# A NaN-ignoring maximum over 512 MB: tiles cut into row pieces, stores moved to the load queue

## The chip, the core and the metric

The kernel runs on one core of one Trainium2 chip. Times are device microseconds of that core. Five engines run side by side, each with its own instruction queue: PE (unused here), ACT, DVE, POOL and SP, which issues the loads. Instructions wait for each other through semaphores.

## The reference

```python
def setup_inputs():
    batch, seq, dim = 32, 2048, 2048
    x = np.random.randn(batch, seq, dim).astype(np.float32)
    mask = np.random.rand(batch, seq, dim) < 0.1
    x[mask] = np.nan
    return {"x": x, "axis": -1}

def reference(x, axis):
    return np.nanmax(x, axis=axis).astype(np.float32)
```

65,536 rows of 2048 floats (8 KB a row, 536.87 MB in all) become 65,536 maxima; a tenth of the input is NaN.

## The kernel before

Each of the 128 partitions takes 512 rows. They are worked on in 14 groups (`GROUPS`): 12 groups of 40 rows a partition in five tiles of 8, one group of 24 (7, 6, 5, 4, 2), one of 8 (2, 2, 1, 1, 1, 1). A tile of 8 rows is 64 KB a partition, 8.39 MB. Tiles come from a pool of three buffers (`io`, `bufs=3`); a load into a buffer waits until the tile that was there is reduced.

A tile goes through four steps, each one instruction over the whole tile:

- SP issues the load (L74).
- ACT changes the upper 16 bits of each float in place, with a Prelu of the negated bits (L77). POOL subtracts the result from a constant, in place, and so brings the bits back (L85). Between them, the two map the upper halves of NaNs to those of a very low number and leave the others as they are.
- DVE takes the maximum of each row into `acc` (L93).

After a group's last tile DVE finds rows that had only NaN (`none`, L101) and puts the NaN back into the result (`fin`, L110); ACT's queue issues the group's store (L113). Each queue runs in the order in which its instructions stand. The framework that builds the program adds the semaphores, and places ACT's store of a group behind the first activation of the next group (the order below shows it).

Of the kernel before, what the change touches and what calls it, by code (L numbers as in the profile page):

```python
# [1 line left out]

# [4 lines left out]

GROUPS = [(40, [8] * 5)] * 12 + [
    (24, [7, 6, 5, 4, 2]),
    (8, [2, 2, 1, 1, 1, 1]),
]

TOP = 0x7F7F
NAN = 0x7FC0
LOW = -129  # L20

EDGE = TOP + 0.25

NONE = -255.0 * 2.0**120


@with_exitstack
def kernel(
    ctx: ExitStack,
    tc: tile.TileContext,  # L30
    x: bass.AP,
    axis: bass.AP,
    out: bass.AP,
):

    nc = tc.nc
    P = nc.NUM_PARTITIONS
    f32, i32 = mybir.dt.float32, mybir.dt.int32
    i16, u16 = mybir.dt.int16, mybir.dt.uint16
    ALU = mybir.AluOpType

    nd = len(x.shape)
    assert axis in (-1, nd - 1), axis  # L50
    D = x.shape[-1]

    xr = x.bitcast(i32).flatten_outer_dims()
    R = xr.shape[0]
    of = out.bitcast(i32).flatten_outer_dims().rearrange("r c -> (r c)")
    assert R == P * sum(s for s, _ in GROUPS)

    io = ctx.enter_context(tc.tile_pool(name="io", bufs=3))
    res = ctx.enter_context(tc.tile_pool(name="res", bufs=3))
    sing = ctx.enter_context(tc.tile_pool(name="sing", bufs=1))  # L60
    top = sing.tile([P, 1], f32)
    nc.vector.memset(top, EDGE)  # L62

    r0 = 0
    for s, cuts in GROUPS:
        assert sum(cuts) == s
        xg = xr[r0 : r0 + P * s].rearrange("(p s) d -> p s d", p=P)
        og = of[r0 : r0 + P * s].rearrange("(p s) -> p s", p=P)
        r0 += P * s
        acc = res.tile([P, s], f32, tag="acc")  # L70
        at = 0
        for c in cuts:
            xt = io.tile([P, c * D], i32, tag="xt")
            nc.sync.dma_start(  # L74
                out=xt, in_=xg[:, at : at + c].rearrange("p c d -> p (c d)")
            )
            nc.scalar.activation(  # L77
                out=xt.bitcast(u16)[:, 1::2],
                in_=xt.bitcast(i16)[:, 1::2],
                func=mybir.ActivationFunctionType.Prelu,  # L80
                bias=top,
                scale=-1.0,
                alpha=float(TOP - LOW) / (EDGE - NAN),
            )
            nc.gpsimd.tensor_scalar(  # L85
                out=xt.bitcast(i16)[:, 1::2],
                in0=xt.bitcast(u16)[:, 1::2],
                scalar1=-1.0,
                scalar2=float(TOP),
                op0=ALU.mult,  # L90
                op1=ALU.add,
            )
            nc.vector.tensor_reduce(  # L93
                out=acc[:, at : at + c],
                in_=xt.bitcast(f32).rearrange("p (c d) -> p c d", c=c),
                axis=mybir.AxisListType.X,
                op=ALU.max,
            )
            at += c
        none = res.tile([P, s], i32, tag="none")  # L100
        nc.vector.tensor_scalar(  # L101
            out=none,
            in0=acc,
            scalar1=NONE,
            scalar2=float(0x00C00000),
            op0=ALU.is_equal,
            op1=ALU.mult,
        )
        fin = res.tile([P, s], i32, tag="fin")
        nc.vector.tensor_tensor(  # L110
            out=fin, in0=acc.bitcast(i32), in1=none, op=ALU.bitwise_or
        )
        nc.scalar.dma_start(out=og, in_=fin)  # L113


# [1 line left out]
_INS = ['x', 'axis']  # L117
_OUTS = [((32, 2048), 'float32')]

_NUMBERS = {'axis': -1}  # L120


# [26 lines left out]
```

## Time and profile before

| | |
|---|---|
| median of 3 runs | 1747.19 us (1747.01 to 1747.41) |
| the profiled execution's own time | 1748.27 us |
| its span, first to last instruction | 1746.5 us |
| busy: ACT, POOL, DVE | 1182.0, 1174.7, 1143.4 us |
| read from HBM | 536.87 MB, 308 GB/s over the span |

A row of the timeline is: start, duration, engine, line, operation, out<-in, number of instructions, and in brackets the idle time ahead of it with what ended it. A row of groups: line, engine, operation, out<-in with shapes, count | busy us, mean ns of one | idle time before, what ended it. `128x16384` is a tile of 8 rows as ACT and POOL see it (upper halves alone), `128x8` its result on DVE. A row of waits: who waited for whom, us in total, times, longest. A row of windows: the window, its length, busy time of DVE, ACT and POOL, granted clock, DMA share, GB/s. A row of DMA issues: out<-in, queue, count, KB each, median us from issue to landing. "SPq" and "ACTq" are the queues of these engines.

### The profile page before, as it was taken

What the parts mean: (1) busy time and instruction counts of PE and PEld (TensorE: products, weight loads), DVE (VectorE), ACT (ScalarE), POOL (GpSimd) and SP (SyncE); (2) the same over time, 40 slices, a digit from 0 to 9 for tenths busy, and PEclk for the clock granted to TensorE, in tenths of its full rate; (3) what the DMA queues carried; (4) which work ended last, traced back from release to release, by engine and by line L of the source; (5) the groups of instructions that cost most, each with busy time, mean ns of one, the idle gap of its engine ahead of it and who ended that gap; (6) DMA issues with size and microseconds to landing.
All of it is one profiled execution on the core that took longest, in us unless ns stands there. A gap on an engine that the chain in (4) does not pass through costs nothing.

```text
span 1746.5 us, 655 instructions
## 1 busy us (share of the span) xinstructions
DVE 1143.4 (65%) x100; ACT 1182.0 (68%) x72; POOL 1174.7 (67%) x75
## 2 busy tenths in 40 slices
DVE  0568585585585585675674774864865856856886
ACT  4865956856857757758668668567577586586553
POOL 0959577587586585595595595595595595595854
DMA  9595976966967867868768669669569669569343
GB/s 420 234 444 246 385 308 269 385 282 294 385 264 312 361 263 338 334 268 360 313 264 384 293 260 408 265 263 429 241 267 410 265 264 428 245 264 411 142 192 144
DMA packets 12244, 537.17 MB, mean 308 GB/s; under 512 B 3152, under 2 KB 3152, under 8 KB 3152
## 3 DMA queue, kind: packets, MB, share of 16 engines
q1 hardware_dynamic: 10224, 536.88, 72.6%
q10 hardware_dynamic: 2016, 0.26, 0.1%
q14 instruction: 4, 0.03, 0.0%
HBM read 536.87 MB, written 0.26 MB: 308 GB/s over the span
## 4 chain that ended last, share of the span: by engine, by line
DVE 26%; POOL 26%; ACT 22%; DMA 19%; issue 6%; ACTq 0%; POOLq 0%; DVEq 0%
POOL xt L85 26%; DVE acc L93 24%; ACT xt L77 22%; DMA xt<-in_x_dram 19%; DVE none L101 2%; ACTq L113 0%; POOLq L144 0%; DVE fin L110 0%; ACTq L77 0%; POOLq L85 0%; DVEq L93 0%
## 5 line engine op out<-in xcount | busy, mean ns | idle before, releaser
L85 POOL TENSOR_SCALAR xt<-xt 128x16384 int16<-128x16384 uint16 (+4 forms) x71 | 1174.5, 16542 | 566.4 <-ACT xt L77 565.6
L77 ACT ACTIVATE xt<-xt,top 128x16384 uint16<-128x16384 int16 (+4 forms) x71 | 1180.7, 16642 | 533.8 <-DMA xt<-in_x_dram 323.1
L93 DVE TENSOR_REDUCE acc<-xt 128x8 f32<-128x16384 f32 (+4 forms) x71 | 1102.6, 15535 | 598.9 <-POOL xt L85 598.9
L101 DVE TENSOR_SCALAR none<-acc 128x40 int32<-128x40 f32 (+2 forms) x14 | 39.1, 2790 | 0.5
L77 ACT ACT_TABLE_LOAD x1 | 1.3, 1283 | 23.0 <-DMA xt<-in_x_dram 23.0
L110 DVE TENSOR_TENSOR fin<-acc,none 128x40 int32<-128x40 int32 (+2 forms) x14 | 2.8, 197 | 0.5
L62 DVE MEMSET top<- 128x1 f32 x1 | 0.1, 59 | 0.8 <-PEq L130 0.8
L130 POOL MEMSET const-float32-0.0<- 128x1 f32 x1 | 0.1, 98 | 0.2 <-issue 0.2
L130 POOL MEMSET const-bfloat16-1.0<- 128x1 bf16 x1 | 0.1, 102 | 0.0
L130 POOL MEMSET const-uint8-127<- 128x1 uint8 x1 | 0.1, 102 | 0.0
L130 POOL MEMSET const-float32-1.0<- 128x1 f32 x1 | 0.1, 98 | 0.0
## 6 DMA issues: line engine op xcount, KB each, us to landing
xt<-in_x_dram SPq DMA_DIRECT2D x1, 7168.0 KB, 19.6
xt<-in_x_dram SPq DMA_DIRECT2D x1, 6144.0 KB, 16.9
xt<-in_x_dram SPq DMA_DIRECT2D x3, 2048.0 KB, 7.3
xt<-in_x_dram SPq DMA_DIRECT2D x1, 5120.0 KB, 14.6
xt<-in_x_dram SPq DMA_DIRECT2D x1, 4096.0 KB, 12.0
xt<-in_x_dram SPq DMA_DIRECT2D x4, 1024.0 KB, 4.7
xt<-in_x_dram SPq DMA_DIRECT2D x60, 22.0
out_dram<-fin ACTq DMA_DIRECT2D x12, 20.0 KB, 19.6
```

The lines of the kernel that those rows point to most:

```text
L62: nc.vector.memset(top, EDGE)
L77: nc.scalar.activation(out=xt.bitcast(u16)[:, 1::2], in_=xt.bitcast(i16)[:, 1::2], func=mybir.ActivationFunctionType.Prelu, bias=top, scal ...
L85: nc.gpsimd.tensor_scalar(out=xt.bitcast(i16)[:, 1::2], in0=xt.bitcast(u16)[:, 1::2], scalar1=-1.0, scalar2=float(TOP), op0=ALU.mult, op1= ...
L93: nc.vector.tensor_reduce(out=acc[:, at : at + c], in_=xt.bitcast(f32).rearrange("p (c d) -> p c d", c=c), axis=mybir.AxisListType.X, op=A ...
L101: nc.vector.tensor_scalar(out=none, in0=acc, scalar1=NONE, scalar2=float(0x00C00000), op0=ALU.is_equal, op1=ALU.mult,)
L110: nc.vector.tensor_tensor(out=fin, in0=acc.bitcast(i32), in1=none, op=ALU.bitwise_or)
L130: nc = _bacc.Bacc("TRN2", target_bir_lowering=False, num_devices=1)
```

## The change

A group is now a list of tiles, a tile a list of loads, a load a list of pieces. The 60 tiles of the first 12 groups stay one load each, but ACT, POOL and DVE work on it in pieces of 3, 3 and 2 rows (`FULL`). The last 32 rows become four groups of one tile each: a full tile; a tile of three loads (2+2, 2, 2 rows); a tile of six loads (2, 2, 1, 1, 1, 1); a tile of eight loads of one row. Stores are kept in a list and issued on SP's queue behind a load, when at least two groups are done; what is left goes out at the end. A Prelu on one number a partition (`warm`) stands ahead of everything on ACT. The three instructions on a piece are those of before, on the view `xp` of its rows.

```diff
-GROUPS = [(40, [8] * 5)] * 12 + [
-    (24, [7, 6, 5, 4, 2]),
-    (8, [2, 2, 1, 1, 1, 1]),
+FULL = [[3, 3, 2]]
+GROUPS = [[FULL] * 5] * 12 + [
+    [FULL],
+    [[[2, 2], [2], [2]]],
+    [[[2], [2], [1], [1], [1], [1]]],
+    [[[1], [1], [1], [1], [1], [1], [1], [1]]],
 ]
+WIDE = 8
...
+    warm = sing.tile([P, 1], f32)
+    nc.scalar.activation(out=warm, in_=top, func=PRELU, alpha=0.5)
 
+    stores = []
...
-        for c in cuts:
-            xt = io.tile([P, c * D], i32, tag="xt")
-            nc.sync.dma_start(
-                out=xt, in_=xg[:, at : at + c].rearrange("p c d -> p (c d)")
-            )
...
+        for tl in g:
+            xt = io.tile([P, WIDE * D], i32, tag="xt")
+            base = at
+            for ld in tl:
+                c = sum(ld)
+                nc.sync.dma_start(
+                    out=xt[:, (at - base) * D : (at - base + c) * D],
+                    in_=xg[:, at * D : (at + c) * D],
+                )
+                if len(stores) > 1:
+                    nc.sync.dma_start(**stores.pop(0))
+                for c in ld:
+                    xp = xt[:, (at - base) * D : (at - base + c) * D]
...
+                    at += c
...
-        nc.scalar.dma_start(out=og, in_=fin)
+        stores.append(dict(out=og, in_=fin))
+    for st in stores:
+        nc.sync.dma_start(**st)
```

Three places show how instructions move. The first is ACT's queue from its start (`xt` is the tile, `fin` the result of a group of 40 rows). Before:

```order
L77 ACT_TABLE_LOAD
L77 ACTIVATE xt<-xt,top 128x16384 x6
L113 DMA out_dram<-fin 128x40
L77 ACTIVATE xt<-xt,top 128x16384 x5
L113 DMA out_dram<-fin 128x40
```

and changed:

```order
L71 ACT_TABLE_LOAD
L71 ACTIVATE warm_66<-top_64 128x1
L94 ACTIVATE xt_69<-xt_69,top_64 128x6144 x2
L94 ACTIVATE xt_69<-xt_69,top_64 128x4096
L94 ACTIVATE xt_80<-xt_80,top_64 128x6144 x2
L94 ACTIVATE xt_80<-xt_80,top_64 128x4096
```

The store is gone from between the activations, a tile is three activations, and the table load does not stand behind the first load any more.

The second is SP's queue at the end of the program. Before (the last loads; there is nothing else on the queue):

```order
L74 DMA xt<-in_x_dram 128x16384 x60
L74 DMA xt<-in_x_dram 128x14336
L74 DMA xt<-in_x_dram 128x12288
L74 DMA xt<-in_x_dram 128x10240
L74 DMA xt<-in_x_dram 128x8192
L74 DMA xt<-in_x_dram 128x4096 x3
L74 DMA xt<-in_x_dram 128x2048 x4
```

and changed, where `xt_799` is tile 60 (the tiles are counted from 0), `xt_816` tile 61, `xt_838` tile 62, `xt_869` tile 63, and `fin_796`, `fin_813`, `fin_835` are the results of the groups that end with tile 59, 60 and 61:

```order
L86 DMA xt_799<-in_x_dram 128x16384
L91 DMA out_0_dram<-fin_735 128x40
L86 DMA xt_816<-in_x_dram 128x8192
L91 DMA out_0_dram<-fin_796 128x40
L86 DMA xt_816<-in_x_dram 128x4096 x2
L86 DMA xt_838<-in_x_dram 128x4096 x2
L91 DMA out_0_dram<-fin_813 128x8
L86 DMA xt_838<-in_x_dram 128x2048 x4
L86 DMA xt_869<-in_x_dram 128x2048 x2
L91 DMA out_0_dram<-fin_835 128x8
L86 DMA xt_869<-in_x_dram 128x2048 x6
L132 DMA out_0_dram<-fin_866 128x8
```

Three stores now stand between loads, one tile or two behind the tile whose result they carry. (A load of 4 or 2 rows is one row here with 8192 or 4096 elements, 2048 a row.)

The third is DVE's queue at the same place, as changed:

```order
L127 TENSOR_TENSOR fin_796<-acc_737,none_794 128x40
L110 TENSOR_REDUCE acc_798<-xt_799 128x3 x2
L110 TENSOR_REDUCE acc_798<-xt_799 128x2
L110 TENSOR_REDUCE acc_815<-xt_816 128x2
L118 TENSOR_SCALAR none_811<-acc_798 128x8
L110 TENSOR_REDUCE acc_815<-xt_816 128x2
L127 TENSOR_TENSOR fin_813<-acc_798,none_811 128x8
L110 TENSOR_REDUCE acc_815<-xt_816 128x2 x2
L110 TENSOR_REDUCE acc_837<-xt_838 128x2
L118 TENSOR_SCALAR none_833<-acc_815 128x8
L110 TENSOR_REDUCE acc_837<-xt_838 128x2
L127 TENSOR_TENSOR fin_835<-acc_815,none_833 128x8
```

`none` and `fin` of a short group stand behind the first and the second reduce of the next tile, where before, with the last two groups,

```order
L93 TENSOR_REDUCE acc_438<-xt_459 128x2
L101 TENSOR_SCALAR none_464<-acc_438 128x24
L110 TENSOR_TENSOR fin_466<-acc_438,none_464 128x24
L93 TENSOR_REDUCE acc_469<-xt_470 128x2
L93 TENSOR_REDUCE acc_469<-xt_475 128x2
```

they stood right behind their own.

More of the change, by code (lines that the diff above doesn't have):

```diff
@@ L47 @@
     ALU = mybir.AluOpType
+    PRELU = mybir.ActivationFunctionType.Prelu
     nd = len(x.shape)
@@ L55 @@
     of = out.bitcast(i32).flatten_outer_dims().rearrange("r c -> (r c)")
-    assert R == P * sum(s for s, _ in GROUPS)
+    rows = [sum(sum(sum(ld) for ld in tl) for tl in g) for g in GROUPS]
+    assert R == P * sum(rows)
     io = ctx.enter_context(tc.tile_pool(name="io", bufs=3))
@@ L62 @@
     nc.vector.memset(top, EDGE)
+    warm = sing.tile([P, 1], f32)
+    nc.scalar.activation(out=warm, in_=top, func=PRELU, alpha=0.5)
+    stores = []
     r0 = 0
-    for s, cuts in GROUPS:
-        assert sum(cuts) == s
-        xg = xr[r0 : r0 + P * s].rearrange("(p s) d -> p s d", p=P)
+    for s, g in zip(rows, GROUPS):
+        xg = xr[r0 : r0 + P * s].rearrange("(p s) d -> p (s d)", p=P)
         og = of[r0 : r0 + P * s].rearrange("(p s) -> p s", p=P)
@@ L71 @@
         at = 0
-        for c in cuts:
-            xt = io.tile([P, c * D], i32, tag="xt")
-            nc.sync.dma_start(
-                out=xt, in_=xg[:, at : at + c].rearrange("p c d -> p (c d)")
-            )
[L77 to L99, printed above, removed]
+        for tl in g:
[11 more added lines that the diff above has]
+                    xp = xt[:, (at - base) * D : (at - base + c) * D]
+                    nc.scalar.activation(
+                        out=xp.bitcast(u16)[:, 1::2],
+                        in_=xp.bitcast(i16)[:, 1::2],
+                        func=PRELU,
+                        bias=top,
+                        scale=-1.0,
+                        alpha=float(TOP - LOW) / (EDGE - NAN),
+                    )
+                    nc.gpsimd.tensor_scalar(
+                        out=xp.bitcast(i16)[:, 1::2],
+                        in0=xp.bitcast(u16)[:, 1::2],
+                        scalar1=-1.0,
+                        scalar2=float(TOP),
+                        op0=ALU.mult,
+                        op1=ALU.add,
+                    )
+                    nc.vector.tensor_reduce(
+                        out=acc[:, at : at + c],
+                        in_=xp.bitcast(f32).rearrange("p (c d) -> p c d", c=c),
+                        axis=mybir.AxisListType.X,
+                        op=ALU.max,
+                    )
+                    at += c
```

## The prediction

> **What bounds the kernel now.** I read the page's busy shares and queues first, then the chain of waits, then the table of waits, then the timeline around the stores.
>
> ```profile
> DVE 1143.4 (65%) x100; ACT 1182.0 (68%) x72; POOL 1174.7 (67%) x75
> q1 hardware_dynamic: 10224, 536.88, 72.6%
> q10 hardware_dynamic: 2016, 0.26, 0.1%
> ...
> 230.97 21.91 DMA xt<-in_x_dram
> ...
> 252.97 18.44 ACT xt L77
> ...
> 271.48 18.58 POOL xt L85
> ...
> 290.08 17.23 DVE acc L93
> ```
>
> Nothing is full: three engines are busy two thirds of the span, the load queue 73%. This stretch of the chain, 76.3 us from the load's issue to the reduce's end, shows why: a tile is loaded whole, then goes through ACT, POOL and DVE whole, and only the reduce's end lets the next load into its buffer. Three buffers share that loop, so a tile cannot take less than 76.3 / 3 = 25.4 us. The loads do wait for the reduces, and ACT waits for something else as well:
>
> ```profile
> SPq L74 <- DVE acc L93: 1676.5, 67, 55.4
> ...
> ACT xt L77 <- DMA xt<-in_x_dram: 323.1, 51, 20.6
> ACT xt L77 <- DVE fin L110: 210.6, 11, 19.2
> ```
>
> The last row is the store on ACT's queue: it stands ahead of the next activation and waits for the group's last reduce. So five tiles take 133.3 us (`none` starts at 174.04 and again at 307.33, below), not 5 x 25.4 = 127.
>
> ```profile
> 157.80 18.32 POOL L85 TENSOR_SCALAR xt<-xt 128x16384 int16<-128x16384 uint16 x1 [1.04 <-ACT xt L77]
> 174.04 2.12 DVE L101 TENSOR_SCALAR none<-acc 128x40 int32<-128x40 f32 x1
> ...
> 307.33 2.26 DVE L101 TENSOR_SCALAR none<-acc 128x40 int32<-128x40 f32 x1
> ...
> 1622.87 29.90 POOL L85 TENSOR_SCALAR xt<-xt 128x14336 int16<-128x14336 uint16 x2
> ...
> 1640.08 12.73 DVE L101 TENSOR_SCALAR none<-acc 128x40 int32<-128x40 f32 x1
> ```
>
> `none` is tiny, yet ends at 176.16 and 1652.81, when POOL's instruction ends (176.12, 1652.77): it is held while POOL works. I need that below.
>
> **The change: pieces.** A tile becomes 3, 3 and 2 rows on each engine. Prices of 8, 2 and 1 rows:
>
> ```profile
> L77 ACT ACTIVATE xt<-xt,top 128x16384 uint16<-128x16384 int16 x60 | 1105.7, 18433 | 474.4 <-DMA xt<-in_x_dram 263.8 <-DVE fin L110 210.6
> L85 POOL TENSOR_SCALAR xt<-xt 128x16384 int16<-128x16384 uint16 x60 | 1099.8, 18331 | 522.5 <-ACT xt L77 522.3
> L93 DVE TENSOR_REDUCE acc<-xt 128x8 f32<-128x16384 f32 x60 | 1033.1, 17218 | 578.1 <-POOL xt L85 578.1
> ...
> L85 POOL TENSOR_SCALAR xt<-xt 128x4096 int16<-128x4096 uint16 x3 | 14.2, 4728 | 11.5 <-ACT xt L77 11.3
> ...
> L93 DVE TENSOR_REDUCE acc<-xt 128x2 f32<-128x4096 f32 x3 | 13.2, 4413 | 7.9 <-POOL xt L85 7.9
> ...
> L77 ACT ACTIVATE xt<-xt,top 128x2048 uint16<-128x2048 int16 x4 | 10.0, 2544 | 9.1 <-DMA xt<-in_x_dram 9.1
> ...
> L85 POOL TENSOR_SCALAR xt<-xt 128x2048 int16<-128x2048 uint16 x4 | 9.8, 2458 | 6.9 <-ACT xt L77 6.7
> L93 DVE TENSOR_REDUCE acc<-xt 128x1 f32<-128x2048 f32 x4 | 9.0, 2280 | 5.7 <-POOL xt L85 5.7
> ```
>
> A straight line through 8 rows and 1 row gives ACT 2.27 us a row + 0.27, POOL 2.27 + 0.19, DVE 2.13 + 0.15. Three rows are then 7.08, 6.99 and 6.55 us; two rows 4.81 (ACT), 4.73, 4.41. A tile costs ACT 18.97, POOL 18.71 (18.95 with some 0.08 between instructions), DVE 17.51: the cut adds 0.3 to 0.5 us per engine and tile.
>
> From a load's landing to the last reduce's end: ACT's first piece 7.08, POOL's first two 13.98, DVE's last two 10.96, handovers 0.3: 32.3 us, where 54 stood. The other pieces run beside these.
>
> With the slowest issue to landing of a load alone (22.16, the first below) the loop is 54.5 us, 18.2 a tile. That is less than ACT and POOL need and less than the transfer needs, so the bound moves.
>
> ```profile
> 0.74 22.16 DMA xt<-in_x_dram
> ...
> 22.97 1.28 ACT L77 ACT_TABLE_LOAD   x1 [22.97 <-DMA xt<-in_x_dram]
> 24.27 36.62 ACT L77 ACTIVATE xt<-xt,top 128x16384 uint16<-128x16384 int16 x2
> ...
> 61.58 18.42 ACT L77 ACTIVATE xt<-xt,top 128x16384 uint16<-128x16384 int16 x1 [0.69 <-DMA xt<-in_x_dram]
> ...
> 119.97 18.39 ACT L77 ACTIVATE xt<-xt,top 128x16384 uint16<-128x16384 int16 x1 [1.31 <-DMA xt<-in_x_dram]
> ...
> 139.30 18.42 ACT L77 ACTIVATE xt<-xt,top 128x16384 uint16<-128x16384 int16 x1 [0.94 <-DMA xt<-in_x_dram]
> ...
> 1.00:61.00 60.00, 0.00 (x0) 37.90 (x3) 18.26 (x1) 1.00 0.98 419
> ```
>
> The load queue's own pace: tile 0 lands at 22.9; the third, queued since the start, lands just ahead of ACT's start at 61.58: 38.6 for two, **19.3 us a tile**. The starts at 119.97 and 139.30, both released by a load, give 19.33. The window of the first 60 us says 419 GB/s, which would be 8.39 MB / 419 = 20.0 us; but a window counts whole packets, so I take 19.33 and keep 20.0 as the upper bound. Against 58.0 for three tiles the loop has 3.5 us to spare, so each load is queued before the one ahead of it is done. POOL has 0.4 us a tile to spare, and the next tile's first piece reaches it just as it is done.
>
> The Trainium skill ("HBM Reference", Specifications) gives about 425 GB/s for a core that streams alone; that would be 19.74 us a tile, an estimate, and 25 us on the sum. Its page "SBUF — State Buffer", Summary, says to reckon 358 GB/s from HBM: an estimate of 23.4 us a tile and some 1530 us in all. The 419 of the window above disagrees with the second.
>
> **Stores moved to the load queue.** ACT no longer waits for `fin`: that takes the 210.6 us off ACT, part of the 26.7 us a tile, so it is not counted twice. In the main stretch a store is issued a whole group after its `fin`, so it waits for nothing; the next load stands behind its 0.45 us issue, covered by the 3.5. On the DMA engines all 14 stores took 0.1% of 1746.5 = 1.7 us, 0.12 each; ten before tile 60 lands cost 1 us. Upper bound: the 1.4 us that a store alone took to land, 14 us.
>
> **`none`** now starts 32.3 us after its tile's landing, while POOL is in the next tile's first piece (26.8 to 33.8), so it is held about 1.5 us; DVE has 19.33 - 17.51 = 1.8 us a tile to spare. Priced at nothing; at worst a whole 6.99 us piece, of which the 3.5 of slack swallow half: 12 x 3.5 = 42.
>
> **Early activation:** the table load (1.3 us) leaves the first tile's path, but the stream behind does not wait for that tile until the loop's slack is used. Nothing.
>
> **The tail.** Count from tile 60's landing (the last full tile). Here the order on the queue bites: three stores now wait for a `fin` that is not there yet, and the loads stand behind them. Rows for what is issued to an idle ring (with two for the rivals):
>
> ```profile
> xt<-in_x_dram SPq DMA_DIRECT2D x3, 2048.0 KB, 7.3
> ...
> xt<-in_x_dram SPq DMA_DIRECT2D x4, 1024.0 KB, 4.7
> xt<-in_x_dram SPq DMA_DIRECT2D x60, 22.0
> out_dram<-fin ACTq DMA_DIRECT2D x12, 20.0 KB, 19.6
> ...
> out_dram<-fin ACTq DMA_DIRECT2D x1, 4.0 KB, 1.4
> ...
> 1741.33 2.29 DVE L93 TENSOR_REDUCE acc<-xt 128x1 f32<-128x2048 f32 x1 [0.26 <-POOL xt L85]
> ...
> 1744.05 0.34 ACTq L113 DMA_DIRECT2D out_dram<-fin  x1
> ```
>
> - Tile 61's four rows are issued when tile 58 is done, at 32.3 - 38.7 = -6.4, and are through at 9.7. The store of tile 59's group waits until 32.3 - 19.3 + 0.4 = 13.4. **The DMA engines idle from 9.7.**
> - Four loads of 2 rows follow at 13.8: the first lands at 21.1 (7.3), the rest 4.9 apart, until 35.8.
> - The next store needs tile 60's `fin`, which DVE now runs behind two reduces of tile 61: 32.3 + 4.4, a hold of `none` behind POOL until about 40.3, 4.4 and 0.2: 44.9. **Idle again, 9 us.**
> - Six single rows: first at 45.4 + 4.7 = 50.1, 2.5 apart, until 62.6.
> - The third store needs four more reduces of 2 rows (17.8): 62.9. Then six single rows, landing 68.1 to 80.4.
> - DVE then has twelve single-row reduces (27.4) and a `none` (about 1.3): the last reduce ends at 91.5, not at 80.4 + 7.5.
> - `none`, `fin` 0.4, and 2.45 from the store's issue to the span's end (1744.05 to 1746.5): **94.4**.
>
> Unhindered, 24 rows would need 24 x 2.42 = 58 us and some 10 more: the waits cost about 25 us.
>
> The Trainium skill ("SBUF — State Buffer", Who interferes with whom) says that a DVE operation with two SBUF inputs contends with a POOL instruction that reads SBUF, and the later one waits; `fin` is such an operation, and at up to one POOL piece of 2 rows (4.73 us) each it would add, as an estimate, 2 us net in this tail. The trace of before cannot show it: POOL stands idle beside `fin`.
>
> **Sum.** 22.9 + 60 x 19.33 = 1182.7; stores 1; tail 94.4: 1278. For boundaries between loads that are less smooth than the first three I add 0.1 us a tile, 6, an estimate between 0 (those three) and 0.7 (the 20.0): **span 1284**. The profiled execution took 1748.27 against its span of 1746.5, the median of the runs is 1.1 lower: 1284 + 1.8 - 1.1 = **1285 us**.
>
> **Rivals.**
>
> - *The stream is slower when it never pauses.* For it: the window's 419 GB/s, and that before paused after every second or third load; against it: the first three loads. At 20.0 a tile +40 less the 6: 1319; with 14 for the stores 1332. That has 0.11. At the 22.0 us which the median of the 60 loads took from issue to landing, start included, +160 less the 6: 1439, chance 0.03. The skill's 358 GB/s lies beyond this end.
> - *DVE does not get its turn between POOL's pieces.* In the rows above `none` ended with POOL's instruction, but POOL had nothing next; now the next piece follows 0.08 later. If `none` needs the 0.4 us gap between two tiles, it is held 13.2 us a group, 9.9 beyond the slack: 12 x 9.9 = 119, 1404. If even that gap is too short, it waits until POOL has run dry, through the two tiles in the other buffers and the one refilled, some 52 us; DVE then sets the pace with 5 x 17.51 + 52 + 0.4 = 140 us a group against 133.3 before: 1680 + 54 + 92, about **1825, slower than before**. It decides from a gap of 0.4 us. `none` ends within 0.04 us of POOL's end, which speaks against both. Chances 0.04 and 0.02.
> - *A store blocks the load queue until it is written.* Stores of 20 KB took 19.6 us in before, sharing engines with a load; if the ring stood that long 12 times, 235 us: 1520. The 1.4 of a store alone speaks against. 0.02.
> - *The change doesn't do what it says:* POOL's first piece waits for ACT's whole tile. The loop stays 76.3 + 1.2, 25.8 a tile, without ACT's hold: 1285 + 60 x 6.5 = 1675. POOL's pieces each have a wait of their own in the order, so 0.02.
>
> **Numbers.** The forecast has 0.76, with its own range of 1270 (no allowance, shorter holds in the tail) to 1305. To leave out 2 in 10 or less I go to 1335, the end of the first rival's bounds: 1270 to 1335. A measurement here tells about 0.2% (3.5 us) from no change; only the port rival's far end is slower (0.02), no case lands within (I keep 0.01 for it), the rest is faster: 0.97.
>
> **What would show it.** Right: DMA share at 95% or more from the start to tile 60; loads 19.3 to 19.5 us apart; ACT idle before a tile, released by the load; `none` at most 7 us; in the last 100 us loads waiting for `fin`, with pauses of about 5 and 10 us. Wrong: pauses of the DMA in the main stretch, POOL busy over 98%, `none` of 13 us or more, or loads over 20 us apart.

## The result and the profile after

| | before | changed |
|---|---|---|
| median | 1747.19 us | **1284.18 us** (1283.97 to 1284.49, 3 runs) |
| span of the profiled execution | 1746.5 us | 1282.3 us |

The ratio is 0.735, with a 95% interval of 0.733 to 0.737. The forecast was 1285 us (1270 to 1335).

The page of the changed kernel, its busy shares, load queue and chain by engine:

```profile
DVE 1142.7 (89%) x234; ACT 1203.3 (94%) x203; POOL 1203.8 (94%) x205
q1 hardware_dynamic: 13536, 537.14, 97.1%
DMA 42%; POOL 23%; DVE 18%; ACT 12%; issue 5%; ACTq 0%; DVEq 0%
```

ACT and POOL work 21 and 29 us longer than before, which is mostly the price of the pieces; the span is 464 us shorter. The load queue went from 72.6% to 97.1%. The waits, of the engines and then of the load queue:

```profile
DVE acc L110 <- POOL xt L102: 135.4, 110, 35.9
ACT xt L94 <- DMA xt<-in_x_dram: 67.0, 63, 20.3
POOL xt L102 <- ACT xt L94: 58.9, 62, 29.3
...
SPq L91 <- DVE fin L127: 65.3, 3, 28.4
```

ACT waits only for loads, some 0.6 us a tile; the row with `fin` is gone from ACT and stands on the load queue, three times, all in the tail. The timeline around the last full tiles, and the windows of the main stretch and the tail:

```profile
22.57 18.68 ACT L94 ACTIVATE xt<-xt,top 128x6144 uint16<-128x6144 int16 x3 [20.34 <-DMA xt<-in_x_dram]
...
1166.47 18.77 ACT L94 ACTIVATE xt<-xt,top 128x6144 uint16<-128x6144 int16 x3 [0.60 <-DMA xt<-in_x_dram]
...
1179.38 0.33 SPq L86 DMA_DIRECT2D xt<-in_x_dram  x1
...
1185.84 46.79 ACT L94 ACTIVATE xt<-xt,top 128x6144 uint16<-128x6144 int16 x9 [0.59 <-DMA xt<-in_x_dram]
1187.84 10.88 DVE L110 TENSOR_REDUCE acc<-xt 128x3 f32<-128x6144 f32 x2 [0.54 <-POOL xt L102]
```

```profile
23.00:1183.00 1160.00, 1046.98 (x200) 1122.41 (x180) 1117.34 (x179) 1.00 1.00 433
1183.00:1282.30 99.30, 95.69 (x34) 78.99 (x22) 86.23 (x23) 1.00 0.62 254
```

Tile 0 starts on ACT at 22.57, tile 60 at 1185.84: 19.39 us a tile. The load of tile 61 is issued at 1179.38, some 6 us before tile 60 has landed. (This time, from the issue of a load to the landing of the load ahead of it, is called its lead below; the "ring" is what the 16 DMA engines still have queued.) Over 1160 us the DMA engines moved 433 GB/s with hardly a pause. Tile 59, which starts at 1166.47, is reduced at 1187.84 + 10.88 = 1198.72, 32.3 us after its landing.

The tail, from DVE and the load queue:

```profile
1198.76 1.32 DVE L118 TENSOR_SCALAR none<-acc 128x40 int32<-128x40 f32 x1
...
1200.34 0.34 SPq L91 DMA_DIRECT2D out_dram<-fin  x1
...
1222.33 4.10 DVE L118 TENSOR_SCALAR none<-acc 128x8 int32<-128x8 f32 x1
...
1230.60 0.56 DVE L127 TENSOR_TENSOR fin<-acc,none 128x8 int32<-128x8 int32 x1
...
1231.19 0.34 SPq L91 DMA_DIRECT2D out_dram<-fin  x1
...
1250.13 0.83 DVE L127 TENSOR_TENSOR fin<-acc,none 128x8 int32<-128x8 int32 x1
...
1250.99 0.34 SPq L91 DMA_DIRECT2D out_dram<-fin  x1
...
1266.15 13.24 DVE L110 TENSOR_REDUCE acc<-xt 128x1 f32<-128x2048 f32 x6
...
1279.42 0.17 DVE L118 TENSOR_SCALAR none<-acc 128x8 int32<-128x8 f32 x1
```

Against the landing of tile 60 (1185.8) the three stores are issued at 14.6, 45.4 and 65.2, where the prediction had 13.4, 44.9 and 62.9; the last reduce ends at 93.6 instead of 91.5.

### The profile page after: what moved, and what is told of

Read it like the earlier page. It is cut to its first block, busy times and chain, and to the rows that moved or that the text cites. A ratio compares the mean times of both kernels' runs of the same rounds, so it can differ in the third digit from the quotient of the medians.

```text
span 1282.3 us, 1065 instructions
## 1 busy us (share of the span) xinstructions
DVE 1142.7 (89%) x234; ACT 1203.3 (94%) x203; POOL 1203.8 (94%) x205
## 3 DMA queue, kind: packets, MB, share of 16 engines
q1 hardware_dynamic: 13536, 537.14, 97.1%
## 4 chain that ended last, share of the span: by engine, by line
DMA 42%; POOL 23%; DVE 18%; ACT 12%; issue 5%; ACTq 0%; DVEq 0%
DMA xt<-in_x_dram 42%; POOL xt L102 23%; DVE acc L110 18%; ACT xt L94 12%; DVE none L118 1%; DVE fin L127 0%; ACTq L94 0%; DVEq L110 0%; DVEq L127 0%
## 5 line engine op out<-in xcount | busy, mean ns | idle before, releaser
L102 POOL TENSOR_SCALAR xt<-xt 128x6144 int16<-128x6144 uint16 (+2 forms) x201 | 1203.6, 5988 | 69.9 <-ACT xt L94 58.9
L94 ACT ACTIVATE xt<-xt,top 128x6144 uint16<-128x6144 int16 (+2 forms) x201 | 1201.8, 6082 | 67.0 <-DMA xt<-in_x_dram 67.0
L110 DVE TENSOR_REDUCE acc<-xt 128x3 f32<-128x6144 f32 (+2 forms) x201 | 1116.0, 5582 | 135.4 <-POOL xt L102 135.4
L118 DVE TENSOR_SCALAR none<-acc 128x40 int32<-128x40 f32 (+1 forms) x16 | 24.4, 1526 | 0.5
L127 DVE TENSOR_TENSOR fin<-acc,none 128x40 int32<-128x40 int32 (+1 forms) x16 | 4.4, 275 | 0.4
## 6 DMA issues: line engine op xcount, KB each, us to landing
out_dram<-fin SPq DMA_DIRECT2D x12, 20.0 KB, 25.5
```

The costliest lines, as they stand in the source:

```text
L94: nc.scalar.activation(out=xp.bitcast(u16)[:, 1::2], in_=xp.bitcast(i16)[:, 1::2], func=PRELU, bias=top, scale=-1.0, alpha=float(TOP - LOW ...
L102: nc.gpsimd.tensor_scalar(out=xp.bitcast(i16)[:, 1::2], in0=xp.bitcast(u16)[:, 1::2], scalar1=-1.0, scalar2=float(TOP), op0=ALU.mult, op1= ...
L110: nc.vector.tensor_reduce(out=acc[:, at : at + c], in_=xp.bitcast(f32).rearrange("p (c d) -> p c d", c=c), axis=mybir.AxisListType.X, op=A ...
L118: nc.vector.tensor_scalar(out=none, in0=acc, scalar1=NONE, scalar2=float(0x00C00000), op0=ALU.is_equal, op1=ALU.mult,)
L127: nc.vector.tensor_tensor(out=fin, in0=acc.bitcast(i32), in1=none, op=ALU.bitwise_or)
```

## The experiments

Each starts from the changed kernel (1284.2 us) and runs beside the kernel before on the same chip, whose medians there were 1748.4 to 1749.8.

### The stores alone, the pieces alone

Stores back on ACT's queue, pieces kept:

```diff
-                if len(stores) > 1:
-                    nc.sync.dma_start(**stores.pop(0))
...
-        stores.append(dict(out=og, in_=fin))
-    for st in stores:
-        nc.sync.dma_start(**st)
+        nc.scalar.dma_start(out=og, in_=fin)
```

> The changed kernel, but with each group's store back on ACT's queue, right after the group; the pieces stay. ACT's order then has the store behind the first piece of the next group. Theory (the hold of ACT is a cost of its own): `fin` comes some 34 us after its tile's landing, so ACT's second piece of the next tile starts 8 us late in each group; ACT has 0.6 us a tile to make that up, so it becomes the bound: 5 x 18.73 + 8 = 102 us a group against 96.9, and the ring runs dry: between 12 x 5 = 60 and 80 us more, 1340 to 1365 us. ACT waits for `fin` about 12 times 8 us. Rival (the pieces alone carry the gain and their slack swallows the hold): within 5 us of the changed kernel's 1284.

Measured: 1355.3 us, 0.775 of before (0.774 to 0.776). Its waits, and the timeline at the first store:

```profile
ACT xt L91 <- DVE fin L124: 123.6, 15, 9.7
ACT xt L91 <- DMA xt<-in_x_dram: 26.0, 10, 20.4
```

```profile
119.48 7.10 ACT L91 ACTIVATE xt<-xt,top 128x6144 uint16<-128x6144 int16 x1 [0.63 <-DMA xt<-in_x_dram]
...
133.96 0.38 ACTq L127 DMA_DIRECT2D out_dram<-fin  x1
134.38 48.90 ACT L91 ACTIVATE xt<-xt,top 128x6144 uint16<-128x6144 int16 x8 [7.80 <-DVE fin L124]
```

ACT does one piece of tile 5, then stands 7.8 us behind the store, which waits for tile 4's `fin`. Then it runs eight pieces without a gap and hardly ever waits for a load any more: ACT has become the bound. The hold costs 71 us; the slack of the pieces does not swallow it.

The other half, whole tiles with the stores on the load queue:

```diff
-FULL = [[3, 3, 2]]
+FULL = [[8]]
```

> The changed kernel, but the 61 full tiles are worked on whole (one piece of 8 rows); stores stay on the load queue, the tail stays. Theory: the loop of load, ACT, POOL and DVE is back at 76.3 us for three tiles, 25.4 a tile, without ACT's hold: 1284 + 60 x (25.4 - 19.39) = 1645, plus some 10 for loads into a ring that has run dry: 1645 to 1665 us. That is 80 to 100 under the kernel before, the share of the stores' move alone. Rival (the stores' move is the larger part): under 1500 us.

Measured: 1662.0 us, 0.951 (0.950 to 0.952). In its chain one round of the loop is as in the kernel before:

```profile
402.62 21.93 DMA xt<-in_x_dram
...
424.64 18.40 ACT xt L94
...
443.12 18.33 POOL xt L102
...
461.47 17.23 DVE acc L110
```

That is 76.1 us for three tiles. So against the kernel before the stores' move brings 86 us and the pieces 393, each with the new tail and the early activation; all together bring 463. The tail's share can be told by the time at which DVE is done with tile 59: 1640.0 before, 1568.0 with the stores moved, 1261.6 with the pieces, 1198.7 with both. Up to there the stores' move brings 72 us, the pieces 378, both 441.

### What sets the pace of the main stretch

Without ACT's, POOL's and `none`'s work (the handling of NaN is left out, and DVE takes the maximum of the words as integers):

```diff
-                    nc.scalar.activation(
...
-                    nc.gpsimd.tensor_scalar(
...
                     nc.vector.tensor_reduce(
-                        out=acc[:, at : at + c],
-                        in_=xp.bitcast(f32).rearrange("p (c d) -> p c d", c=c),
+                        out=acc[:, at : at + c].bitcast(i32),
+                        in_=xp.rearrange("p (c d) -> p c d", c=c),
```

> The changed kernel without ACT's, POOL's and `none`'s work: it leaves out all handling of NaN, and DVE takes the maximum of the words as integers, in the same pieces; loads, buffers and stores are as in the changed kernel. Theory (in the changed kernel's main stretch the load queue alone sets the pace): tiles still land 19.33 to 19.40 us apart, tile 60 at 1183 to 1187 us, and only the tail is shorter, since nothing runs behind the loads: 59 us for 24 rows and some 5 at the end: 1245 to 1252 us. Rival (ACT and POOL, 94% busy, hold the loads back or slow them down): tiles land closer together, or the time falls below 1235 us.

Measured: 1260.3 us, over the expected 1252. The window of the main stretch and the tail on DVE:

```profile
23.00:1183.00 1160.00, 1041.45 (x191) 0.00 (x0) 0.00 (x0) 1.00 1.00 433
```

```profile
1185.80 21.66 DVE L94 TENSOR_REDUCE acc<-xt 128x3 int32<-128x6144 int32 x4 [1.80 <-DMA xt<-in_x_dram]
...
1238.14 17.63 DVE L94 TENSOR_REDUCE acc<-xt 128x1 int32<-128x2048 int32 x8
```

The main stretch is the same to the digit: 433 GB/s, and work on tile 60 starts at 1185.80, where it was 1185.84. ACT and POOL, 94% busy, cost it nothing. The miss is in the tail: DVE begins tile 60 when it lands, needs 17 us for it, and then has 24 rows at 2.2 us to go, 53 us; it ends at 1255.8, whatever the loads do. I had counted only the loads.

How far POOL stands behind the load queue, in pieces of one row:

```diff
-FULL = [[3, 3, 2]]
+FULL = [[1] * 8]
```

> The changed kernel, but the 61 full tiles are worked on in eight pieces of one row. POOL then costs 8 x (2.46 + 0.08) = 20.3 us a tile, ACT 8 x 2.45 = 19.6, DVE 8 x 2.20 = 17.6, and a tile is done sooner after its landing. Theory (POOL stands just 0.4 us a tile behind the load queue, so the fixed price of a piece shows once it is over the queue's 19.39): POOL is the bound, 60 x (20.3 - 19.39) = 55 more, less some 12 of a shorter end: 1325 to 1340 us, POOL busy over 97%. Rival (the load queue stays the bound, pieces are free): 1270 to 1285 us.

Measured: 1335.3 us, 0.764 (0.763 to 0.765). POOL's group, and the main stretch:

```profile
L102 POOL TENSOR_SCALAR xt<-xt 128x2048 int16<-128x2048 uint16 x500 | 1234.0, 2468 | 64.3 <-ACT xt L94 24.7
```

```profile
23.00:1183.00 1160.00, 1040.74 (x476) 1117.76 (x461) 1121.85 (x455) 1.00 0.99 417
```

Eight pieces at 2.47 + 0.08 are 20.4 us; tiles land 20.2 us apart, and POOL is busy 96.7% of the stretch. Its 64.3 us of idle time are 24.7 at the start and the 0.08 between 500 pieces: it never waits in between, so it is the bound. The pieces are not free: with 3, 3 and 2 POOL's price for them just fits under the queue's 19.39. The 97% that I expected was missed by little.

### How early a load must be queued

Two pieces instead of three:

```diff
-FULL = [[3, 3, 2]]
+FULL = [[4, 4]]
```

> The changed kernel, but the full tiles are worked on in pieces of 4 and 4 rows. From landing to the last reduce's end this takes 9.35 + 2 x 9.26 + 8.68 + 0.3 = 36.9 us instead of 32.3 (measured 31.5); a load is then issued 38.7 - 36.9 = 1.8 us before the ring runs dry instead of 6. Theory of the prediction (any lead of a us or more is enough, and what lies above it is worth nothing): 1283 to 1288 us, since POOL and ACT save 0.2 a tile. Rival (the boundaries between loads cost when the lead is near 2 us, as they did in the kernel before, where the engines of the ring don't end together): 0.3 to 1 us a tile, 1300 to 1345 us.

(The 31.5 us named there is a slip: the trace has 32.3.) Measured: 1336.8 us (1331.6 to 1339.1), 0.764 (0.763 to 0.766), **53 us more than with three**. The windows of its main stretch, and two successive loads on the timeline:

```profile
23.00:1183.00 1160.00, 1002.68 (x135) 1066.09 (x115) 1057.63 (x114) 1.00 0.98 415
```

```profile
300.49 0.33 SPq L86 DMA_DIRECT2D xt<-in_x_dram  x1
...
304.20 18.59 ACT L94 ACTIVATE xt<-xt,top 128x8192 uint16<-128x8192 int16 x2 [0.92 <-DMA xt<-in_x_dram]
...
321.51 39.43 SPq L86 DMA_DIRECT2D xt<-in_x_dram  x3
...
323.66 18.68 ACT L94 ACTIVATE xt<-xt,top 128x8192 uint16<-128x8192 int16 x2 [0.87 <-DMA xt<-in_x_dram]
...
346.13 18.57 ACT L94 ACTIVATE xt<-xt,top 128x8192 uint16<-128x8192 int16 x2 [3.79 <-DMA xt<-in_x_dram]
```

The tile that starts on ACT at 323.66 was issued at 300.49, 3.7 us before its predecessor started: it comes 19.46 us after it. The next was issued at 321.51, 2.2 us before: it comes 22.47 us after, 3.1 us late. Both were queued before the load ahead had landed, and the second is late all the same. The packets of this trace show where the time goes. A load's first packet starts about 1 us after its issue (in the idle ring at the start: issued at 0.74, first packet at 1.75), and by then engines have run dry: at 322.4 only 5 of the 16 DMA engines work on a load, where all 16 stay at work from 300 to 306, around the load that came in time. Eleven engines start on the late load 0.95 to 1.1 us after its issue, others only 1.9 to 3.1 us after; why these start so late stays open. ACT and POOL have gaps in this kernel (120 and 134 us of idle time), so it is not they who hold it.

To tell the lead from the size of the pieces, the same pieces with the tile in two loads:

```diff
-FULL = [[3, 3, 2]]
+FULL = [[4], [4]]
```

> As the run with pieces of 4 and 4 rows, but each full tile is also loaded in two loads of 4 rows, so that work on it starts when its first half has landed: from the tile's landing to the last reduce's end some 27 us instead of 37, and a load is issued some 11 us before the ring runs dry instead of 2 to 4. The engines' work is the same to the instruction. Theory (the 52 us that 4 and 4 cost over 3, 3 and 2 came from the short lead): the pace is back at 19.4 to 19.5 us a tile, 1278 to 1292 us. Rival (pieces of 4 rows themselves cost, by their size on ACT, POOL and DVE): 1325 to 1340 us as before.

Measured: 1279.6 us, 0.731 (0.730 to 0.733). The main stretch:

```profile
23.00:1183.00 1160.00, 1040.28 (x141) 1117.97 (x120) 1105.93 (x120) 1.00 1.00 432
```

The instructions on ACT, POOL and DVE are the same as with one load of 8 rows; what has changed is the size of a load, when work on a tile starts and ends, and so how early the next load is queued: by the landings the lead is 11.2 us or more, where it was 1.7 to 5.4. 57 us are gone, some 48 of them before tile 60 has landed (1190.8 against 1238.7), the rest in the tail. So pieces of 4 rows are not the cost, and loads of 8 rows aren't either, since the changed kernel has them too. The lead is what is left.

### The tail and the start

All stores of the last six groups behind the last load (with more result buffers, so that no `fin` waits for a store):

```diff
-    res = ctx.enter_context(tc.tile_pool(name="res", bufs=3))
+    res = ctx.enter_context(tc.tile_pool(name="res", bufs=8))
...
-                if len(stores) > 1:
+                if len(stores) > 1 and s == 40:
```

> The changed kernel, but the stores of the last six groups are all issued behind the last load, so no load of the tail waits for a `fin` (the result buffers are more, so that nothing waits for a store). Theory of the prediction (the waits on the load queue cost the tail about 25 us): 1284 - 25, so 1255 to 1265 us. Rival, from the profile after (POOL is 26 us behind tile 60's landing and then has 24 rows to go, 4 + 2 pieces of 2 rows at 4.81 and 12 of one row at 2.54 = 59 us, so it ends some 85 us after that landing whatever the loads do): the loads land earlier, ACT runs ahead, and the end moves by 0 to 4 us: 1280 to 1284 us.

Measured: 1284.4 us, the same as the changed kernel. From its timeline:

```profile
1179.93 45.58 SPq L86 DMA_DIRECT2D xt<-in_x_dram  x16
...
1186.01 75.74 ACT L94 ACTIVATE xt<-xt,top 128x6144 uint16<-128x6144 int16 x21 [0.57 <-DMA xt<-in_x_dram]
...
1193.23 78.46 POOL L102 TENSOR_SCALAR xt<-xt 128x6144 int16<-128x6144 uint16 x21 [0.34 <-ACT xt L94]
...
1266.49 13.24 DVE L110 TENSOR_REDUCE acc<-xt 128x1 f32<-128x2048 f32 x6
```

The loads go out without waiting for a result, ACT and POOL run on in one piece, ACT to 1261.8 instead of 1271.1, POOL to 1271.7 instead of 1273.9, and yet DVE's last reduces begin at 1266.49 instead of 1266.15. In the changed kernel the waits on the load queue are there (65.3 us), and they cost nothing: DVE ends last, and it has work all along.

Without the early activation:

```diff
-    warm = sing.tile([P, 1], f32)
-    nc.scalar.activation(out=warm, in_=top, func=PRELU, alpha=0.5)
```

> The changed kernel without the early activation. Theory: the table load of 1.3 us then stands behind the first tile's landing; the fourth load has 6 us of lead, so the stream does not see it: the same time within 1 us, 1283 to 1285 us. Rival (the start is on the path): 1.3 us more, 1285.5.

Measured: 1284.4 us (1284.18 to 1284.49), the same. The table load is off the path either way.

### A faster version

If the tail is as long as the engines stand behind the last full tile, they have to stand closer:

```diff
-FULL = [[3, 3, 2]]
+FULL = [[2, 2], [2, 2]]
 GROUPS = [[FULL] * 5] * 12 + [
-    [FULL],
-    [[[2, 2], [2], [2]]],
-    [[[2], [2], [1], [1], [1], [1]]],
-    [[[1], [1], [1], [1], [1], [1], [1], [1]]],
+    [FULL, FULL, FULL, [[2], [2], [2], [1], [1]]],
 ]
...
-                if len(stores) > 1:
+                if len(stores) > 1 and s == 40:
```

(and four result buffers).

> A try at a faster kernel: full tiles as two loads of 4 rows, worked on in four pieces of 2 rows; the last 32 rows a partition are one group of three such tiles and one of loads of 2, 2, 2, 1 and 1 rows; the last three stores behind the last load. If the tail is set by how far POOL and DVE stand behind the last full tile's landing (26 and 31 us in the changed kernel), they now stand some 9 us closer, and the single result at the end saves two holds of `none` and `fin`: 1270 to 1278 us. POOL needs 4 x 4.83 = 19.3 us a tile, as much as the queue, so against it: POOL becomes the bound, or smaller packets cost the loads 0.1 us a tile and more, and the time is 1280 to 1295.

Measured: **1272.5 us** (1272.40 to 1272.54), 0.728 of before (0.727 to 0.729), 11.8 us less than the changed kernel without the early activation beside it (1284.4). Its page:

```profile
DVE 1142.2 (90%) x284; ACT 1219.7 (96%) x259; POOL 1213.7 (96%) x261
q1 hardware_dynamic: 20736, 537.14, 98.3%
```

The load queue is at 98.3%, ACT and POOL at 96%. How much of the 11.8 us comes from the closer engines and how much from the single result at the end was not taken apart. The run with the stores last gives a bound, an estimate: POOL ends there at 1271.7, and with one row more on DVE (2.3 us) the last reduce could not end before 1274.0, where it ended at 1279.7. So the holds of `none` and `fin` are worth 5.7 us at most, and the rest is due to the other changes.

## Why the prediction was right, and where it was not

- **The loop and its new bound: right.** Landing to the last reduce's end was worked out as 32.3 us and is 32.3. The pace is the load queue's, shown by the run without ACT and POOL: the same 433 GB/s.
- **The pace of the stream: right, the allowance too large.** 19.39 us a tile instead of 19.33 and 0.1 more. Tile 60 landed at 1185.8; the sum had 1182.7, with stores and allowance 1189.7. Choosing the arrival of the first loads over the window's 419 GB/s was right; the same stretch counted over 1160 us gives 433. The first rival falls. Of the Trainium skill's two figures, the 425 GB/s of "HBM Reference", Specifications, is near, and the 358 of "SBUF — State Buffer", Summary, does not hold for this lone core.
- **The slack of the loop: right here; to fall short of it costs more than the sum says.** The prediction's loop of 54.5 us has 22.16 for a load from issue to landing, 2.8 more than its 19.33 in the stream; the 3.5 us to spare against 58.0 are thus a lead of 6.3 us, and the trace has 6.2 to 7.4. With two pieces the same sum gives 36.9 + 22.16 = 59.1, over the 58.0 by 1.1: 19.7 us a tile, some 21 us in all. The run lost 53, at 20.27 us a tile. (What was expected of that run, that a lead of one us is enough, left the 2.8 us out.) In that run 11 loads with a lead under 2.3 us landed 20.0 to 22.7 us after the load ahead, 23 with 4 us or more 19.3 to 20.0. The trace of before had it already: of its back-to-back loads, most of them queued 2 to 3 us ahead, several came 21 to 22 us after their predecessors. That the 16 engines end a load apart is not enough for a loss: in the changed kernel they report its landing 0.5 to 2.1 us apart, and by the packets they idle between two loads only beside a store, 0.1 us on average.
- **The stores: right, and shown apart.** The prediction took ACT's hold for a part of the 26.7 us a tile and did not count it twice. Up to the end of tile 59 on DVE the hold is worth 72 us where tiles are whole and 63 where they are pieces (1261.6 against 1198.7). On the load queue a store takes 25.5 us to land but costs next to nothing: by the trace's packets the loads beside one end 19.42 us apart, the others 19.35. So the rival by which a store blocks the queue falls as well.
- **`none`: right.** In the main stretch it lasts 1.2 to 1.4 us; some 1.5 were worked out. It gets its turn between two POOL pieces 0.08 us apart, so the rival by which it waits for a gap falls; in the tail it was held 4.1 us at most.
- **The tail: the events right to 1 to 2 us, the conclusion wrong.** "The waits cost about 25 us" compared with 24 rows of loads and "some 10 more", as if the engines were up to date when tile 60 lands. They are not: DVE ends tile 60 32.3 us after its landing and then has 24 rows at 2.2 us and the holds of `none` and `fin`: that alone is over 85 us. With the waits gone the time is the same. The sum held because its last step followed DVE's queue rather than the loads. The tail took 96.5 us, 94.4 were forecast.
- **`fin` behind POOL: as the Trainium skill said.** Its page "SBUF — State Buffer", Who interferes with whom, has a DVE operation with two SBUF inputs contend with a POOL instruction that reads SBUF. The trace agrees: in the tail `fin` lasted 0.56, 0.83 and 0.42 us where 0.17 to 0.20 is its length, and ended each time within 0.05 us of the end of POOL's instruction. The three holds come to 1.3 us, the estimate was 2.
- **The early activation: nothing, as forecast.**

So the middle of the forecast came out 1 us off, and that is luck in part, since errors cancel: the main stretch was 3.9 us shorter than the sum with its allowance, the tail 2.1 longer.

## What to carry to other kernels

Where a few buffers go round through several engines, cutting the engines' work into pieces shortens the loop without changing the transfers; work out the new loop against the next bound, and check that each piece's fixed price still fits under it. Keep some microseconds of lead, not just a positive number (here 6 us were enough and 2 were not): a load needs time from its issue to its first packets; loading a tile in two parts buys them without a fourth buffer. And before a wait in a tail is priced, follow the engine that ends last: if it has a backlog as long as the tail, the waits ahead of it are free.

## What was not expected of the hardware

Loads queued 2 us before the load ahead had landed came up to 3 us late, those with 6 us of lead did not: a load's first packets start about 1 us after its issue, and not on all 16 DMA engines at once, so engines idle in between. And a DVE operation that waits for POOL is let in between two POOL instructions that follow each other within 0.08 us, every time (15 of 15 held ones in the changed kernel).
